# Moving the out-projection's weight preparation from SyncE's DMA queue to GpSimd's in a hybrid decoder layer

## The chip, the cores and the metric

The kernel runs on one core of a Trainium2 chip. A core has TensorE (matrix products), VectorE, ScalarE and GpSimd, and SyncE, which here does nothing but issue DMAs. In the profile they are PE (PEld for its weight loads), DVE, ACT, POOL and SP; "SPq" is SyncE's queue. DMAs are issued from SyncE's queue and, where they add to what is stored, from GpSimd's. The metric is the device time of one execution in microseconds (us): 1060.5 as the median of three runs, from 1057.32 to 1062.9.

## The reference

One layer on x of 1024 rows by 1024 columns, in float32. The rows are normalized and multiplied by one wide matrix w_in, whose columns give all inputs of two groups of heads. Eight heads of differential attention take the difference of two causal softmaxes over the values. Four heads of gated linear attention (GLA) run in chunks of 64 rows. Each head's output is normalized and gated, and both groups lie side by side as 2048 columns that w_out takes back to 1024:

```
h = rms_norm(x, pre_g);  z = h @ w_in
qa, ka, va, ga, qb, kb, vb, gb, gk_low = split_columns(z)
oa = rms_norm(diff_attention(qa, ka, va, lam), subln_g) * (1 - lam_init) * silu(ga)
ob = rms_norm(gla_chunked(qb, kb, vb, log_a), gla_g) * silu(gb)
y = concatenate([oa, ob]) @ w_out
return x + rms_norm(y, post_g)
```

The change is about the last product, and there about the rows 1024 to 2047 of w_out, which belong to GLA ("wg" below), and the rows 0 to 1023, which belong to attention ("wo").

## The kernel before, in words

**Numbers.** Every float32 operand of a product is split in two, a rounded high part (a ScalarE copy or cast to the type float32r) and the rest (a VectorE subtraction), and a product is three products: high by high, low by high, high by low. So each operand needs one cast and one subtraction before TensorE may read it.

**Seven products instead of eight.** Both the projection with w_in and GLA's part of the out-projection cut their matrices into two by two blocks and use Winograd's scheme with seven block products, numbered 1 to 7. Some products take a block as it is (for w_out: 1, 2, 3), the others take sums of blocks (4, 5, 6, 7). The matching operands of the left side are `mixe[n]`: for GLA's outputs, n = 1, 2, 4 come straight from the heads, and n = 3, 5, 6, 7 are sums that are built in DRAM tensors `lefts[n]` by DMAs that add (lines 955 to 963 and `add_left`, line 978).

**Stages.** (1) x is loaded, normalized, transposed and split; the first columns of w_in are loaded beside it. `load_early` (line 235) loads two pairs of column blocks ahead; the pair 4 uses the buffer of pair 2, so its load waits until that has been read. (2) The projection is a list `order` of 196 steps, one block product of a pair of column blocks each; `go(n)` (line 681) runs n steps, and each step prepares the weights of the next ones (`make_weights`, line 288: the cast is line 325, the subtraction line 326), multiplies, and takes what is done through ScalarE and VectorE (`take`, line 357; the snapshot of a product that is used twice is line 437) to DRAM. (3) From step 86 on a second stream, `fill`, runs beside it, one yield a step: GLA, head by head (`gla`, line 854), and then `gla_sums` (line 982), which loads the sums `lefts[n]`, splits them and stores them as `mixe[n]`. Its buffers are six named ones (`k0`, `q0`, `k1`, `q1`, `ks0`, `ks1`), two for each of n = 5, 6, 3, and the same six later hold attention's k, q and ks. (4) Attention and the out-projection run together (`merge`, line 1118): the scores, the values, and `out_early` (line 1430), which multiplies GLA's outputs by the w_out blocks in 28 units j, seven block products of four row tiles each.

**The out-projection's weights** are prepared in stage 2 and 3, once in each step behind step 41 (`wo_step`, line 652):

- *Copies and sums.* `weight_sums` (line 593) makes the four sums of w_out blocks in DRAM, each in four row tiles k: a plain DMA copies one block into `wsd[n][k]` (line 601, from SyncE), and a DMA that adds puts the other one on top (`add_weights`, line 610, from GpSimd). Sums 6 and 4 add another sum, 5 and 6 of the same k.
- *Loads.* A list `wo_todo` of jobs: 12 blocks, 16 sums, 16 tiles of the wo rows, and 4 tiles of the left sum 7. A job loads 128 x 512 numbers into a buffer `wo_raw` (line 677, from SyncE), and two steps later ScalarE casts it (line 640, or 643 with a sign), VectorE subtracts in place (641, 644), and two DMAs store both parts (`wgd`, `wod`, or for the left sum `mixe` by `store_left`, line 646). Two tags share this out, `t4` and `gup`; a tag comes free two steps after its split, and one step after it from step 86 on, when `gup` is given to GLA's states.
- *Use.* `gla_weights(n)` (line 1061) loads the four parts of block n from `wgd` into buffers of the projection's left operand, which are free once the last product that reads them is done: blocks 2, 4, 1 and then 6 at the end of the projection (lines 1100 to 1106), and blocks 7 and 5 (at j = 8) and 3 (at j = 16) inside `out_early`, where the first four tiles of the wo rows follow at j = 20.

**What sets the order.** The code is traced in the order written, and a scheduler then orders each engine's queue: among the instructions whose inputs and buffers it expects to be there, the one traced first goes first. So an instruction that waits for nothing may go far ahead of its place in the code. Three things hold it back: a buffer that isn't free, `tc.keep_in_program_order(ins)`, which ties an instruction to the one traced before it on its engine, and `with tc.issue_after(ins):`, which puts what the block traces on the engine of `ins` behind `ins` in that engine's queue. A queue, once ordered, is served strictly in order on the chip: an instruction that waits holds up all behind it.

GpSimd's other work before attention is small: clearing constants, scaling tiles of x (line 492), one addition for the first operand (line 552), a mask for each half of each GLA head (line 873), and the DMAs that add. In attention it scales the second softmax (line 1223), gates the outputs (line 1315) and issues the adding DMAs of the results (lines 1476, 1496 and 1644).

Of the kernel before, what the change touches and what calls it, by code (L numbers as in the profile page):

```python
# [31 lines left out]
def hymba_kernel(  # L32
# [255 lines left out]
    def make_weights(i):  # L288
        p, n = order[i]
        if wide(p) and p % 2:  # L290
            ws[i] = ws_wide[p - 1, n]
            return
        if p in early and n < 3:
            src = early[p][n - 1]
        else:
            fetch_raw(p, n, i)
            if wide(p):
                (b11, b21), (b12, b22) = ([raws[q].get(kh) for kh in range(2)] for q in (p, p + 1))
            else:
                top, bot = raws[p][0], raws[p][1]  # L300
                b11, b12 = top[:, :, :P], top[:, :, P:]
                b21, b22 = bot[:, :, :P], bot[:, :, P:]


            def sub(dst, a, b):
                dve.tensor_tensor(dst, a, b, ALU.subtract)  # L306
                return dst

            if n == 5:
                src = sub(b11, b12, b11)  # L310
            elif n == 6:
                src = sub(b11, b22, b11)
            elif n == 4:
                src = sub(b21, b21, b11)
            elif n == 7:
                src = sub(b12, b22, b12)
            else:
                src = {1: b11, 2: b21, 3: b22}[n]
        if wide(p):
            w = [ap.tile([P, HB, 256], F32R, tag="ring", name="w", bufs=NRING) for _ in range(2)]  # L320
            ws_wide[p, n] = w
        else:
            w2 = ap.tile([P, 2, HB, P], F32R, tag="ring", name="w", bufs=NRING)
            w = [w2[:, 0], w2[:, 1]]
        act.copy(w[0], src)  # L325
        dve.tensor_tensor(w[1], src, fp(w[0]), ALU.subtract)  # L326
        ws[i] = w

# [264 lines left out]
    def weight_sums():  # L593

        adds = []
        for k in range(HB):
            for n, src, more in (
# [3 lines left out]
                sp.dma_start(wsd[n][k], src)  # L601
# [8 lines left out]
    def add_weights(n, k, more):  # L610
        pool.dma_start(wsd[n][k], more, accum_op=ALU.add, max_dma_last_dim=2048)
        summed.add((n, k))
# [9 lines left out]
    wo_open, wo_free, wo_now = [], {"t4": 0, "gup": 0}, [0]  # L622
# [29 lines left out]
    def wo_step():  # L652
# [3 lines left out]
        if wo_open and wo_open[0][0] <= now - 2:  # L656
# [3 lines left out]
            split(hi, lo, raw, -1.0 if (kind, n) == ("block", 2) else 1.0)  # L660
            if tag in wo_free:
                wo_free[tag] = now + len(wo_free)
# [8 lines left out]
        if tags and wo_todo and wo_ready(*wo_todo[0]):  # L671
# [5 lines left out]
            sp.dma_start(raw, wo_source(*job))  # L677
# [176 lines left out]
    def gla(g):  # L854

        u = None
        for half in range(2):
# [30 lines left out]
            if (g, half) == (3, 0):  # L888
                add_left(0, 3, 6)
            us = [u]  # L890
# [91 lines left out]
    def gla_sums():  # L982
# [4 lines left out]
        units, open_units = [(n, i) for i in range(2) for n in (5, 6, 3)], []  # L987
        add_left(1, 6, 5)
        for now in range(10):
            if now == 2:  # L990
                add_left(1, 3, 6)
            if open_units and open_units[0][0] <= now - 2:
# [7 lines left out]
            if units and (units[0][1] == 0 or now > 3):  # L1000
# [33 lines left out]
    del wo_free["gup"]  # L1034
# [26 lines left out]
    def gla_weights(n):  # L1061
        wg[n] = []
        for i in range(2):
# [4 lines left out]
            for t in range(2):  # L1068
                ins = sp.dma_start(fp(parts[t]), wgd[n][i][t])
                if n == 6:  # L1070
                    tc.keep_in_program_order(ins)
            wg[n].append(parts)
# [27 lines left out]
    for n in (2, 4, 1):  # L1100
        gla_weights(n)
# [4 lines left out]
    gla_weights(6)  # L1106
# [323 lines left out]
    def out_early():  # L1430
# [3 lines left out]
        for j, (n, i) in enumerate(U):  # L1434
# [6 lines left out]
            if j == 8:  # L1441
                gla_weights(7)
                gla_weights(5)
            if j == 16:
                gla_weights(3)
            if j == 20:
                for e in range(4):
                    weights(e)
# [259 lines left out]
```

## Time and profile before

| what | value |
|---|---|
| three runs, median | 1060.5 us |
| the profiled execution | 1057.74 us |
| its span, first to last instruction | 1056.0 us |
| mean granted TensorE clock | 0.967 |
| DMA packets, bytes, rate | 187379, 273.96 MB, mean 259 GB/s |
| SyncE's queue (hardware_dynamic) | 176480 packets, 253.00 MB, 72.3% of 16 engines |
| GpSimd's queue (software_dynamic) | 10816 packets, 19.93 MB, 11.8% of 16 engines |

A row of the timeline gives the start in us, the duration in us, the engine, the line of the kernel, and the operation with what it writes and reads; "x4" means four instructions merged, and brackets hold the idle time before it and what ended that. A row of the waits gives who waited for whom: us in total, how often, and the longest. A row of stretches gives the busy time of each engine with the number of instructions, the granted clock as a share of full speed, the share of the 16 transfer engines that was busy (it can pass 1 a little, since it is a sum of the times that packets took), and the rate. In the chain of waits each piece is followed back from the last instruction to what released it. DMA-issuing instructions of SyncE aren't counted as busy. An idle engine costs nothing unless it is the one that the others wait for.

### The profile page before, as it was taken

How to read it: one execution, taken by the hardware profiler on the slowest of the kernel's cores; microseconds unless marked ns; L12 is line 12 of the kernel's file. 1: busy time of each engine (PE TensorE's matmuls, PEld its weight loads, DVE VectorE, ACT ScalarE, POOL GpSimd, SP SyncE). 2: the span in 40 equal slices, each digit the busy share in tenths (PEclk: the TensorE clock that was granted, in tenths of full speed). 3: DMA queues.
4: the chain of work that ended last, by engine and by line, in shares of the span. 5: the costliest groups of instructions: out<-in, count | busy, mean ns of one | idle time of the engine just before them, and what ended most of it. 6: DMA issues, size and time to landing. Idle time of an engine off the chain costs nothing.

```text
span 1056.0 us, 16013 instructions
## 1 busy us (share of the span) xinstructions
PE 963.9 (91%) x5290; PEld 828.5 (78%) x5290; DVE 749.5 (71%) x1471; ACT 615.5 (58%) x1194; POOL 168.9 (16%) x182
## 2 busy tenths in 40 slices
PE   6759999999899998999998899818999999999997
PEld 5758988888789986998787787616888888888786
DVE  7856588889776674666765777406798888988555
ACT  8432265478357444535554775305688777887773
POOL 5420000000000010000200000001234334434311
PEclk9979999999999998999999999958999999999999
DMA  9984256867877987996979879999999999997667
GB/s 346 283 192 130 89 154 202 297 208 269 287 264 224 294 234 240 316 285 226 308 218 279 263 221 320 358 310 296 341 347 315 369 362 290 303 272 195 136 177 156
DMA packets 187379, 273.96 MB, mean 259 GB/s; under 512 B 19632, under 2 KB 98480, under 8 KB 187200
## 3 DMA queue, kind: packets, MB, share of 16 engines
q1 hardware_dynamic: 176480, 253.00, 72.3%
q0 software_dynamic: 10816, 19.93, 11.8%
q8 instruction: 42, 0.69, 0.3%
q14 instruction: 41, 0.34, 0.1%
HBM read 164.34 MB, written 122.16 MB: 271 GB/s over the span
## 4 chain that ended last, share of the span: by engine, by line
PE 50%; DMA 22%; DVE 10%; issue 7%; ACT 5%; SPq 3%; POOL 1%; DVEq 0%; ACTq 0%; POOLq 0%
PE x L127 10%; PE ypart L127 9%; PE y L127 6%; PE z L127 6%; PE sc L127 6%; PE yps L127 4%; PE po L127 4%; PE wtr L130 2%; DMA left_d<-go 2%; DMA w_early<-in_w_in_dram 2%; DMA wo_raw<-in_w_out_dram 2%; DMA wg_hi<-wg_d 2%; DMA wo_d<-wo_raw 2%; DVE w L326 1%; DMA mixe<-wo_raw 1%
## 5 line engine op out<-in xcount | busy, mean ns | idle before, releaser
L325 ACT CAST w<-w_raw 128x512 fp32r<-128x512 f32 (+1 forms) x164 | 111.1, 685 | 68.0 <-PE y L127 25.9
L326 DVE TENSOR_TENSOR w<-w_raw,w 128x512 fp32r<-128x512 f32 (+1 forms) x164 | 126.3, 778 | 30.8 <-ACT w L325 21.2
L1217 ACT ACTIVATE p<-p,stt 128x896 f32<-128x896 f32 (+7 forms) x128 | 99.3, 776 | 61.5 <-DVE stt L1207 59.6
L1207 DVE CUSTOM_DVE_ANT_0 p<-sc,maskt 128x512 f32<-128x512 f32 (+3 forms) x128 | 74.4, 585 | 48.4 <-PE sc L127 47.8
L127 PE MATMUL x<-s_hi,w 128*128 128x512 f32 x320 | 81.9, 399 | 9.7 <-ACT s L437 9.7
L306 DVE TENSOR_TENSOR w_raw<-w_raw 128x512 f32<-128x512 f32 (+1 forms) x96 | 76.1, 793 | 18.1 <-DMA w_raw<-in_w_in_dram 16.7
L437 ACT COPY s<-x 128x512 f32<-128x512 f32 x84 | 48.9, 583 | 68.0 <-PE x L127 65.7
L1223 POOL TENSOR_SCALAR p<-p,stt,lam 128x1024 f32<-128x1024 f32 (+3 forms) x64 | 56.8, 887 | 190.0 <-DVE stt L1222 186.6
L127 PE MATMUL sc<-ks,q 128*128 128x512 f32 (+1 forms) x192 | 66.8, 351 | 22.1 <-DMA ks<-k_d 22.1
L127 PE MATMUL z<-s_hi,w 128*128 128x512 f32 x320 | 81.5, 398 | 2.8 <-DVE c L450 2.8
L127 PE MATMUL y<-h_hi,w 128*128 128x512 f32 x320 | 81.7, 398 | 2.2 <-DVE w L326 1.9
L873 POOL TENSOR_SCALAR_AFFINE_SELECT gan<-gan 128x512 f32<-128x512 f32 x8 | 14.5, 1808 | 411.2 <-ACT gan L872 411.2
L127 PE MATMUL ypart<-wg_hi,m_in 128*128 128x512 f32 x224 | 73.8, 411 | 6.8 <-issue 6.8
L127 PEld LDWEIGHTS x<-s_hi,w 128*128 128x128 f32 x320 | 60.3, 191 | 24.4 <-ACT s L437 12.2
L640 ACT CAST wo_hi<-wo_raw 128x512 fp32r<-128x512 f32 x44 | 27.2, 619 | 87.6 <-DMA wo_raw<-in_w_out_dram 55.8
L127 PEld LDWEIGHTS z<-s_hi,w 128*128 128x128 f32 x320 | 60.4, 191 | 15.9 <-DVE c L450 3.6
L127 PEld LDWEIGHTS y<-h_hi,w 128*128 128x128 f32 x320 | 60.6, 191 | 15.4 <-DVE w L326 2.3
L641 DVE TENSOR_TENSOR wo_raw<-wo_raw,wo_hi 128x512 fp32r<-128x512 f32 x44 | 30.4, 691 | 59.6 <-ACT wo_hi L640 59.4
L127 PE MATMUL sc<-k,q 128*128 128x512 f32 (+1 forms) x192 | 69.7, 368 | 0.6 <-DVE stt L1207 0.6
L127 PE MATMUL x<-h_hi,w 128*128 128x512 f32 x160 | 41.6, 404 | 19.0 <-ACT w L325 19.0
L127 PEld LDWEIGHTS sc<-ks,q 128*128 128x128 f32 x192 | 36.7, 191 | 27.8 <-issue 22.3
L1266 DVE TENSOR_TENSOR wt_lo<-wtr,wt_hi 128x512 fp32r<-128x512 f32 (+1 forms) x80 | 50.5, 633 | 7.0 <-ACT wt_hi L1265 6.8
(242 smaller groups left out, 2395.9 us busy)
## 6 DMA issues: line engine op xcount, KB each, us to landing
w_raw<-in_w_in_dram SPq DMA_DIRECT2D x56, 512.0 KB, 5.2
m_in<-mixe SPq DMA_DIRECT2D x28, 512.0 KB, 7.0
q<-q_d SPq DMA_DIRECT2D x32, 256.0 KB, 6.5
k<-k_d SPq DMA_DIRECT2D x32, 256.0 KB, 7.4
ks<-k_d SPq DMA_DIRECT2D x64, 128.0 KB, 6.7
v<-v_d SPq DMA_DIRECT2D x16, 512.0 KB, 8.5
y_d<-yst POOLq DMA_DIRECT2D x32, 256.0 KB, 7.0
wo_raw<-in_w_out_dram SPq DMA_DIRECT2D x28, 256.0 KB, 3.5
```

Source lines behind the costliest of these rows:

```text
L127: tc.keep_in_program_order(pe.matmul(*a, **k))
L130: tc.keep_in_program_order(pe.transpose(dst, src, ident))
L306: dve.tensor_tensor(dst, a, b, ALU.subtract)
L325: act.copy(w[0], src)
L326: dve.tensor_tensor(w[1], src, fp(w[0]), ALU.subtract)
L437: act.copy(b[k], ps)
L640: act.copy(hi, src)
L641: dve.tensor_tensor(lo, src, fp(hi), ALU.subtract)
L1207: ins = dve.tensor_tensor_reduce(p[:, a:e], sc[:, : e - a], maskt[:, NZ + P - (e - a) :] if last else maskt[:, : e - a], 1.0, 3e38 if i == ...
L1217: act.activation(p[:, :n], p[:, :n], AF.Exp, bias=st[:, m : m + 1], scale=-1.0, accum_out=st[:, 2 + m : 3 + m],)
L1223: pool.tensor_scalar(p1[:, :n], p1[:, :n], st[:, 5:6], lam, ALU.mult, ALU.mult)
L1266: dve.tensor_tensor(lo[:, :n], pt[:, :n], fp(hi[:, :n]), ALU.subtract)
```

## The change

Four things are changed.

1. The copies of the weight sums (line 601), the adding DMAs (611), the loads of `wo_raw` (677) and the loads of blocks 2, 4, 1 and 6 (1069) are issued from GpSimd's queue. The first three stand inside `with tc.issue_after(last_cast[0])`, where `last_cast` is the latest cast of `make_weights` (line 325), a ScalarE instruction.
2. `gup` becomes two tags, so that with `t4` three loads can be under way until GLA starts. A split follows its load by three steps instead of two, a tag comes free one step after its split, and with more than one tag no load is made in every third step.
3. The left sums 5, 6 and 3 of the first half become six more jobs of `wo_todo`, in tiles of 128 x 512; `gla_sums` keeps the second half, with starts at its steps 1, 3 and 5 and splits three steps later, in nine steps instead of ten.
4. In `out_early` the loads of blocks 7, 5 and 3 are issued in halves at j = 8 and 9, 10 and 11, 16 and 17, and those of the wo rows one at a time at j = 20 to 23.

```diff
-        act.copy(w[0], src)
+        last_cast[:] = [act.copy(w[0], src).ins]
...
-                sp.dma_start(wsd[n][k], src)
+                with tc.issue_after(last_cast[0]):
+                    pool.dma_start(wsd[n][k], src)
...
     def add_weights(n, k, more):
-        pool.dma_start(wsd[n][k], more, accum_op=ALU.add, max_dma_last_dim=2048)
+        with tc.issue_after(last_cast[0]):
+            pool.dma_start(wsd[n][k], more, accum_op=ALU.add, max_dma_last_dim=2048)
...
     wo_todo += [("left", 7, k) for k in range(HB)]
-    wo_open, wo_free, wo_now = [], {"t4": 0, "gup": 0}, [0]
+    wo_todo += [("left", n, k) for n in (5, 6, 3) for k in range(2)]
+    wo_open, wo_free, wo_now = [], {"t4": 0, "gup0": 0, "gup1": 0}, [0]
...
-        if wo_open and wo_open[0][0] <= now - 2:
+        if wo_open and wo_open[0][0] <= now - 3:
...
-            split(hi, lo, raw, -1.0 if (kind, n) == ("block", 2) else 1.0)
+            split(hi, lo, raw, -1.0 if (kind, n) in (("block", 2), ("left", 6)) else 1.0)
             if tag in wo_free:
-                wo_free[tag] = now + len(wo_free)
+                wo_free[tag] = now + 1
...
-        if tags and wo_todo and wo_ready(*wo_todo[0]):
+        if tags and wo_todo and wo_ready(*wo_todo[0]) and (len(wo_free) == 1 or now % 3):
...
-            sp.dma_start(raw, wo_source(*job))
+            with tc.issue_after(last_cast[0]):
+                pool.dma_start(raw, wo_source(*job))
...
             if (g, half) == (3, 0):
                 add_left(0, 3, 6)
+                left_done.update(((5, 0), (6, 0), (3, 0)))
...
-        units, open_units = [(n, i) for i in range(2) for n in (5, 6, 3)], []
+        units, open_units = [(n, 1) for n in (5, 6, 3)], []
         add_left(1, 6, 5)
-        for now in range(10):
-            if now == 2:
+        for now in range(9):
+            if now == 1:
                 add_left(1, 3, 6)
-            if open_units and open_units[0][0] <= now - 2:
+            if open_units and open_units[0][0] <= now - 3:
...
-            if units and (units[0][1] == 0 or now > 3):
+            if units and (now in (1, 3, 5)):
...
-    del wo_free["gup"]
+    del wo_free["gup0"], wo_free["gup1"]
...
-    def gla_weights(n):
-        wg[n] = []
-        for i in range(2):
+    def gla_weights(n, engine=sp, halves=(0, 1)):
+        for i in halves:
...
-                ins = sp.dma_start(fp(parts[t]), wgd[n][i][t])
+                ins = engine.dma_start(fp(parts[t]), wgd[n][i][t])
...
     for n in (2, 4, 1):
-        gla_weights(n)
+        gla_weights(n, pool)
...
-    gla_weights(6)
+    gla_weights(6, pool)
...
-            if j == 8:
-                gla_weights(7)
-                gla_weights(5)
-            if j == 16:
-                gla_weights(3)
-            if j == 20:
-                for e in range(4):
-                    weights(e)
+            for k, m in ((8, 7), (10, 5), (16, 3)):
+                if j in (k, k + 1):
+                    gla_weights(m, halves=(j - k,))
+            if 20 <= j < 24:
+                weights(j - 20)
```

3 lines of the change are left out of this document (2 added, 1 removed).

## The prediction

> **What bounds the kernel now.** First the page's busy line and slices, which say where TensorE rests.
>
> ```profile
> PE 963.9 (91%) x5290; PEld 828.5 (78%) x5290; DVE 749.5 (71%) x1471; ACT 615.5 (58%) x1194; POOL 168.9 (16%) x182
> ...
> PE   6759999999899998999998899818999999999997
> ...
> PEclk9979999999999998999999999958999999999999
> ```
>
> Each digit is 26.4 us (the clock's digits begin right behind its name). TensorE is busy 91% of the span; it rests in the first three slices and in one near 700 us. The same by stretches (columns: width, then PE, PEld, DVE, ACT and POOL busy, granted clock, DMA share, GB/s):
>
> ```profile
> 105.60:400.00 294.40, 290.25 (x1645) 254.90 (x1644) 223.70 (x350) 160.85 (x273) 5.96 (x4) 1.00 0.73 229
> 400.00:640.00 240.00, 225.37 (x1262) 194.86 (x1261) 162.59 (x250) 129.94 (x232) 17.71 (x12) 0.98 0.86 262
> ...
> 680.00:720.00 40.00, 11.58 (x29) 8.44 (x28) 5.07 (x10) 2.45 (x4) 0.00 (x0) 0.54 0.94 317
> 720.00:1056.00 336.00, 324.27 (x1681) 271.65 (x1680) 264.74 (x714) 250.53 (x564) 112.05 (x122) 1.00 0.91 274
> ```
>
> So three places can move: the start; the projection from 105.6 to 640 (294.4 - 290.25 = 4.2 and 240 - 225.4 = 14.6, together 18.8 us of rest); and the **seam** to attention at 680 to 720 (28.4 us of rest, at a granted clock of 0.54). Attention rests 11.7 us in 336. What TensorE waited for, the longest rows of each place (total, times, longest):
>
> ```profile
> PE x L127 <- ACT w L325: 19.0, 1, 19.0
> ```
> ```profile
> PE x L127 <- ACT s L437: 9.7, 5, 3.1
> ```
> ```profile
> PE sc L127 <- DMA ks<-k_d: 22.1, 2, 21.6
> PE ypart L127 <- issue: 6.8, 1, 6.8
> ```
>
> At the start the cast of line 325 stands in front of a load; in the projection snapshots (line 437) come late; at the seam the first scores wait 21.6 us for ks. Who issues what: the instructions that write ws_d (duration min/median/max in ns, first and last start in us), and the SyncE queue's timeline at both places (start, us, merged rows):
>
> ```profile
> L601 SPq DMA_DIRECT2D ws_d<-in_w_out_dram x16: 490/596/1667, 18.8 to 34.0; - x16
> ...
> L611 POOL DMA_DIRECT2D ws_d<-in_w_out_dram x8: 802/914/1682, 29.2 to 43.8; - x8
> ```
> ```profile
> 34.64 9.37 SPq L1452 DMA_DIRECT2D out_dram<-in_x_dram  x6
> 45.56 2.45 SPq L246 DMA_DIRECT2D w_early<-in_w_in_dram  x2
> ```
> ```profile
> 668.06 0.33 SPq L1069 DMA_DIRECT2D wg_hi<-wg_d  x1
> 668.70 0.37 SPq L1005 DMA_DIRECT2D left<-left_d  x1
> ...
> 680.41 1.54 SPq L1095 DMA_DIRECT2D m_in<-mixe  x2
> ...
> 695.67 0.53 SPq L1069 DMA_DIRECT2D wg_hi<-wg_d  x1
> ...
> 697.72 7.27 SPq L377 DMA_DIRECT2D q_d<-qk_st  x8
> ...
> 710.18 5.07 SPq L1026 DMA_DIRECT2D ks<-k_d  x8
> ```
>
> Two things are to be seen. What has no input is issued as soon as its queue is free: the copies of the weight sums, which the code writes behind step 41 of 196, go at 18.8 us, and the copies of line 1452, written inside attention, at 34.6. And at the seam ks stands last in a queue that issues without a pause.
>
> **The change, part by part.**
>
> *Does "behind casts" hold?* The helper that queues work behind an instruction ties only instructions of that instruction's own engine. Every older use in the kernel (lines 255, 1157, 1205, 1288, 1487, 1636) names one of the same engine; line 255 nests two, for ScalarE and VectorE. The new uses name a ScalarE cast around a GpSimd DMA, so I read them as empty. Then the copies go as soon as GpSimd is free, and its timeline says when that is:
>
> ```profile
> 2.19 0.28 POOL L75 TENSOR_SCALAR_AFFINE_SELECT maskt<-maskt 128x128 f32<-128x128 f32 x1
> ...
> 23.79 5.47 POOL L492 TENSOR_SCALAR xt<-xt,ssq 128x1024 f32<-128x1024 f32 x4 [2.26 <-ACT h_hi L531]
> 29.19 2.73 POOL L611 DMA_DIRECT2D ws_d<-in_w_out_dram  x3
> ...
> 67.83 3.33 POOL L611 DMA_DIRECT2D ws_d<-ws_d  x4
> ```
>
> So they start at 2.5 us beside the loads of x and w_in, not at 18.8.
>
> *Start.* The chain of waits, the sizes (KB each, us to landing) and three stretches:
>
> ```profile
> 30.32 0.87 PE xT L130 x8
> ...
> 45.56 18.15 DMA w_early<-in_w_in_dram
> ...
> 64.40 4.69 PE x L127 x12
> ```
> ```profile
> w_raw<-in_w_in_dram SPq DMA_DIRECT2D x56, 512.0 KB, 5.2
> ...
> ws_d<-in_w_out_dram SPq DMA_DIRECT2D x16, 256.0 KB, 7.5
> ```
> ```profile
> 20.00:25.00 5.00, 5.00 (x43) 5.00 (x42) 5.00 (x12) 4.17 (x9) 2.74 (x3) 1.00 1.10 374
> ...
> 60.00:65.00 5.00, 0.60 (x2) 0.50 (x3) 0.62 (x2) 1.27 (x3) 0.00 (x0) 0.50 1.00 282
> 65.00:70.00 5.00, 5.00 (x17) 3.98 (x16) 5.00 (x9) 3.11 (x6) 3.06 (x5) 0.70 0.28 64
> ```
>
> The DMA share is at its full value until 65 us and then falls to 0.28: the backlog ends just when the second w_early lands (45.56 + 18.15 = 63.7), and TensorE goes on at 64.4. Loss: the 16 copies of 256 KB are 4.2 MB, which at 374 GB/s delay x and w_in by 11 us if all stand ahead of them, by none if none do; I take 6, the middle. Gain: on a clear queue w_early would take the 5.2 us of a w_raw load of twice its size, 13 us less. But the bytes stay the same, and the late adds (67.8 us) now come earlier too, so the gain lies between 0 and 13; I take 3, because the backlog should empty about when it did. Net **+3**, with ends at -13 and +11.
>
> The Trainium skill says in "DMA: Bandwidth & Descriptors" (SWDGE vs HWDGE vs iDMA) that DMAs of GpSimd and of SyncE feed different internal queues of each transfer engine, served in turn. No run here shows that yet; by that rule x would have half the rate while copies stand, the loss would be nearer to 11 than to 0, and the start would cost about 8 instead of 3.
>
> *Projection.* What ScalarE waited for between 105 and 640 us, and the split of one block (durations in ns):
>
> ```profile
> ACT wo_hi L640 <- DMA wo_raw<-in_w_out_dram: 55.8, 14, 7.1
> ...
> ACT wo_hi L640 <- DMA wo_raw<-ws_d: 14.8, 5, 7.1
> ```
> ```profile
> L640 ACT CAST wo_hi<-wo_raw x44: 602/621/625, 178.9 to 591.4; 128x512 fp32r<-128x512 f32 x44
> L641 DVE TENSOR_TENSOR wo_raw<-wo_raw,wo_hi x44: 678/692/697, 179.6 to 592.0; 128x512 fp32r<-128x512 f32 x44
> ```
>
> ScalarE stands 70.6 us in front of raw blocks that come late, and behind it stand the snapshots that TensorE waits for. The load now has three steps of lead for two, one more buffer until GLA, and a queue without SyncE's stores ahead of it. Price: 16 copies, 54 loads (the 48 of before and six new left ones) and 16 weight loads of the seam are 86 issues more on GpSimd, at the 0.91 us of line 611 some 79 us, on an engine busy 168.9 of 1056. That is hidden as long as nothing useful waits in the queue. What stands behind a load that waits for its buffer are the eight masks of GLA (line 873), read five steps of that stream later, and the sums of the left blocks:
>
> ```profile
> 639.12 1.14 POOL L980 DMA_DIRECT2D left_d<-left_d  x1 [7.46 <-DMA left_d<-left_d]
> ```
>
> The last of these is read by the left load at 668.70, so 29 us of cover stand there. Gain: from 0 to all 18.8 us of rest; a loss isn't excluded if masks come late, with the same amount as its bound. The waits on line 437 are half of the rest (9.7), and not all are raw's; I take **-6**. With one buffer (from GLA on) a turn takes four steps for three, but more turns are done before GLA: the same work. The six left jobs moved to this stream are six casts of 0.62 us and six subtractions of 0.69 in place of three twice as wide: nothing, beside 225 us of TensorE in 240.
>
> *Seam.* Between 668.06 and 680.41 SyncE issues twelve block loads and one left load (0.37): 12.0 us go; the four from 695.67 to 697.72 are 2.0. If ks keeps its place it goes 14 us sooner. If it may also pass the q and k stores, since the left block that held its buffer no longer follows another one there, all of 21.6 + 6.8 = 28.4 us can go. Against that stand the bytes:
>
> ```profile
> 680.00:700.00 20.00, 8.20 (x21) 5.68 (x19) 3.61 (x6) 1.52 (x3) 0.00 (x0) 0.59 1.03 375
> 700.00:720.00 20.00, 3.38 (x8) 2.76 (x9) 1.46 (x4) 0.93 (x1) 0.00 (x0) 0.50 0.85 259
> ```
>
> To 700 us the transfer engines are full. Only behind that is there room: 375 - 259 GB/s over the 16 us to ks are 1.9 MB, 5 us. So the gain is 5 to 28; I take **-12**, near the issues taken away. Late next are block 2's weights and the first m_in for ypart, then v.
>
> The same page says, in Issuing engines are not separate DMA queues, that all DMAs share the 16 engines and a second issuer saves only issue time. The share of 1.03 up to 700 agrees; by it alone the seam gives 5 and not 12.
>
> *Later blocks in halves.* The issues of blocks 7, 5, 3 and of the rows are spread over the next units; each is read two units of work or more later, and attention rests 11.7 us in all: 0. Were a half late, it would cost a landing, some 5 us.
>
> **Sum.** 3 - 6 - 12 + 0 = -15. The profiled run took 1057.74 us (the span of 1056.0 and 1.7 around it), so 1042.7; it lies 2.8 under the median of 1060.5, and the forecast for the median is **1045 us**.
>
> **Rivals.**
>
> *The order holds after all*, and the copies go behind step 41. For it speaks the plain wording of the edit, against it that the engines differ. The start then loses nothing and gains most of 13, say 12: -12 - 6 - 12 = -30, 1030 us. Chance 0.12.
>
> *The seam is bound by bytes*, and who issues is nothing. For it: 375 GB/s; against: 259 at the end. Seam -5, the start +3, and a projection that the sooner writes slow, -3: -5, 1055 us. Chance 0.22, half "faster", half "same".
>
> *GpSimd's queue stalls the start*, and it ends slower. The adds wait for their copies, and adds onto sums for earlier adds. If most are queued ahead of the scaling of x tiles 4 to 7 (23.79; TensorE transposes them at 30.32), the scaling waits for the backlog. Ended at about 60 instead of 64, it would put the transposes 30 us late, less 5 to 13 regained at w_early: +17 to +25, about +21. With -6 and -12 that is +3, with the seam at its 5 us +10: 1064 to 1071. It decides from the point where the start costs more than 18. Against it: before, the adds stand behind that scaling (29.19). Chance 0.20.
>
> *The forecast*: 0.46, with an own range of 1035 to 1054.
>
> **How the numbers follow.** About 0.5% is what a measurement can tell from no change: 1055.2 and 1065.8. Faster 0.46 + 0.12 + 0.11 = 0.69, same 0.11, slower 0.20. The range reaches into both far rivals, and leaves out the lower part of the first and the upper part of the last: 1027 to 1068.
>
> **What would show it.** Start: line 601 on GpSimd before 20 us, the scaling of xt later than 23.8, TensorE's restart near 67; if line 601 first goes behind 100 us, the order held. Projection: ScalarE's wait at line 640 under 20 us. Seam: no line 1069 on SyncE before 700 us, and the first score 12 us sooner after the last projection product. The forecast is wrong if a mask or a left sum becomes what TensorE waits for, if the start's backlog lasts beyond 75 us, or if ks still stands last at the seam.

## The result: 0.9% slower, and the profile after

The changed kernel takes 1068.86 us (median of 12 runs, 1061.52 to 1074.52), the kernel before 1058.32 in the same comparison (12 runs, 1054.94 to 1062.9): a ratio of 1.0091, with an interval of 1.0063 to 1.012. The profiled execution took 1062.62 us, 6.2 less than the median; a second profile, below, shows which stretch differs between two executions.

First the page of the changed kernel: busy times, TensorE's slices (26.5 us each) and the transfer engines' slices.

```profile
PE 968.8 (91%) x5290; PEld 831.7 (78%) x5290; DVE 747.9 (71%) x1474; ACT 617.6 (58%) x1197; POOL 207.9 (20%) x268
...
PE   3869999989998999999999989574999999999997
...
DMA  9984246877997869888989759998999999997667
```

GpSimd has 86 instructions more, as counted. TensorE begins later (a 3 where a 6 stood), and the hole near 700 is shallower but wider: 5, 7, 4 for 8, 1, 8. To see what is gained and lost, the span is cut at two places that every version of this kernel has: the first of GLA's products (`pa`) and the end of the last one (`gms`). Stretches of the kernel before, with the columns of the prediction's:

```profile
0.00:300.90 300.90, 268.97 (x1496) 234.03 (x1497) 227.99 (x367) 156.79 (x268) 32.92 (x44) 0.97 0.74 227
300.90:616.80 315.90, 300.26 (x1834) 266.72 (x1834) 210.18 (x319) 169.24 (x297) 20.42 (x13) 0.98 0.84 259
616.80:1056.00 439.20, 394.64 (x1963) 327.75 (x1961) 311.35 (x786) 289.47 (x630) 115.55 (x125) 0.96 0.92 282
```

The same stretches of the changed kernel:

```profile
0.00:309.60 309.60, 273.34 (x1496) 236.98 (x1497) 226.54 (x367) 158.08 (x268) 54.22 (x87) 0.97 0.74 229
309.60:621.70 312.10, 299.57 (x1833) 266.40 (x1834) 209.64 (x320) 170.02 (x299) 27.79 (x37) 0.99 0.83 256
621.70:1060.60 438.90, 395.86 (x1962) 328.33 (x1961) 311.67 (x787) 289.56 (x632) 125.92 (x144) 0.96 0.91 281
```

TensorE's products agree to one (1496, 1833, 1962), so these are the same pieces of work. The way to GLA takes 8.7 us more, GLA's stretch 3.8 less in this execution, and all that follows takes 438.9 us for 439.2, although at the seam inside it the wait for ks went. That last pair of numbers is the first to explain.

**The seam.** What TensorE waited for from 640 us on, in the changed kernel:

```profile
PE ypart L127 <- DMA m_in<-mixe: 16.5, 2, 14.3
PE x L127 <- ACT s L439: 11.8, 1, 11.8
PE sc L127 <- DMA ks<-k_d: 2.7, 2, 1.9
```

The 21.6 us for ks are 1.9; instead a snapshot is 11.8 us late ahead of them, and an m_in 14.3 us behind them. The queues show why, GpSimd's, ScalarE's and SyncE's in turn:

```profile
653.88 1.09 POOL L1075 DMA_DIRECT2D wg_hi<-wg_d  x2 [3.64 <-PE x L127]
...
666.54 0.53 POOL L1075 DMA_DIRECT2D wg_lo<-wg_d  x1 [1.37 <-PE x L127]
```
```profile
677.39 1.04 ACT L645 CAST left_hi<-left 128x1024 fp32r<-128x1024 f32 x1 [12.70 <-DMA left<-left_d]
```
```profile
659.20 0.45 SPq L1012 DMA_DIRECT2D left<-left_d  x1
...
660.33 13.07 SPq L652 DMA_DIRECT2D mixe<-left  x2
...
704.93 5.04 SPq L379 DMA_DIRECT2D k_d<-qk_st  x8
...
720.53 0.54 SPq L1101 DMA_DIRECT2D m_in<-mixe  x1
```

A left load is issued at 659.20, in the middle of the twelve block loads (6 MB) that GpSimd now issues between 653.88 and 667.07, and it lands at 677.4, after 18 us; ScalarE stands in front of its cast, and the snapshot behind it. Later the third m_in is issued at 720.53, behind 24 stores of q and k. One long wait for ks has become two, for other loads.

**The start.** The copies' row, the first raw load, then SyncE's first loads of w_in, ScalarE near 61 us and TensorE near 66:

```profile
L604 POOL DMA_DIRECT2D ws_d<-in_w_out_dram x16: 526/558/1098, 2.2 to 34.7; - x16
```
```profile
3.50 0.60 POOL L683 DMA_DIRECT2D wo_raw<-in_w_out_dram  x1
```
```profile
3.22 8.35 SPq L204 DMA_DIRECT2D w_raw<-in_w_in_dram  x2
```
```profile
61.46 0.62 ACT L325 CAST w<-w_early 128x512 fp32r<-128x512 f32 x1 [3.19 <-DMA w_early<-in_w_in_dram]
...
62.93 0.68 ACT L533 ACTIVATE h_hi<-xT,pre_g 128x512 fp32r<-128x512 f32 x1
```
```profile
66.07 3.76 PE L127 MATMUL y<-w,h_hi 128*128 128x256 f32 x16 [7.14 <-DVE s L577]
```

The copies go from 2.2 us on, so the helper's block was empty, as read. The first three raw loads go among them, at 3.50 to 6.18 us; before, SyncE issued them among its copies, at 19.48 to 24.57 us. Two loads of w_in hold SyncE's queue 8.35 us, and the first product comes at 22.65 us (13.59 before). What sets the end of the stage stands in ScalarE's queue: a cast of w_early that waits for its load is now ordered in front of the last activations of h (62.93), and TensorE rests 7.1 us for what hangs on them. Pair 4 begins at 71.33 us for 64.40.

### The profile page after: what moved, and what is told of

It reads as the page before. It is cut to its first block, busy times and chain, and to the rows that moved or that the text cites. A ratio compares the mean times of both kernels' runs of the same rounds, so it can differ in the third digit from the quotient of the medians.

```text
span 1060.6 us, 16114 instructions
## 1 busy us (share of the span) xinstructions
PE 968.8 (91%) x5290; PEld 831.7 (78%) x5290; DVE 747.9 (71%) x1474; ACT 617.6 (58%) x1197; POOL 207.9 (20%) x268
## 5 line engine op out<-in xcount | busy, mean ns | idle before, releaser
L127 PE MATMUL x<-s_hi,w 128*128 128x512 f32 x320 | 86.6, 416 | 24.0 <-ACT s L439 23.9
L127 PEld LDWEIGHTS x<-s_hi,w 128*128 128x128 f32 x320 | 62.5, 199 | 40.6 <-ACT s L439 27.8
L683 POOL DMA_DIRECT2D wo_raw<-in_w_out_dram x28 | 15.4, 552 | 326.4 <-DMA wg_d<-wo_raw 133.4
L645 ACT CAST wo_hi<-wo_raw 128x512 fp32r<-128x512 f32 x48 | 29.6, 619 | 80.6 <-DMA wo_raw<-in_w_out_dram 27.7
L646 DVE TENSOR_TENSOR wo_raw<-wo_raw,wo_hi 128x512 fp32r<-128x512 f32 x48 | 32.9, 688 | 58.6 <-ACT wo_hi L645 58.6
L127 PEld LDWEIGHTS ypart<-wg_hi,m_in 128*128 128x128 f32 x224 | 40.0, 194 | 22.1 <-issue 14.7
L1232 DVE SCALAR_TENSOR_TENSOR p<-p,stt,p 128x1024 f32<-128x1024 f32 (+3 forms) x64 | 52.8, 824 | 4.1 <-POOL p L1229 3.8
```

The lines of the kernel that those rows point to most:

```text
L127: tc.keep_in_program_order(pe.matmul(*a, **k))
L645: act.copy(hi, src)
L646: dve.tensor_tensor(lo, src, fp(hi), ALU.subtract)
L1232: dve.scalar_tensor_tensor(p0[:, :n], p0[:, :n], st[:, 4:5], p1[:, :n], ALU.mult, ALU.subtract)
```

## The experiments

The first theory after these traces: GpSimd's copies cost the start, its block loads cost the end of the projection, and its raw loads are what helps (ScalarE's waits for raw blocks between 105 and 640 us, those for left blocks counted in both, fell from 76.8 us to 42.9; without them from 70.6 to 34.9). The rival: the timetable of the casts costs, whoever issues. Both were wrong on the raw loads. Medians (of 4 to 12 runs), ratios to the kernel before as it was timed beside each, with their intervals, and the three stretches of each profile (to GLA, GLA, the rest), us:

| kernel | median | ratio | to GLA | GLA | rest |
|---|---|---|---|---|---|
| before | 1058.3 | | 300.9 | 315.9 | 439.2 |
| after | 1068.9 | 1.0091 [1.0063, 1.012] | 309.6 | 312.1 | 438.9 |
| after_again | one run: 1072.1 | | 309.7 | 321.9 | 438.5 |
| wg_on_sync | 1071.4 | 1.0125 [1.0092, 1.0158] | 309.4 | 316.9 | 442.8 |
| copies_on_sync | 1064.4 | 1.0056 [1.0035, 1.0076] | 304.2 | 319.8 | 437.6 |
| copies_late | 1063.9 | 1.0052 [1.0027, 1.0077] | 301.1 | 317.3 | 437.6 |
| m_in_early | 1067.4 | 1.0089 [1.0061, 1.0116] | 309.0 | 317.9 | 444.5 |
| raw_on_sync | 1044.1 | 0.9859 [0.9829, 0.9889] | 302.2 | 304.7 | 439.7 |
| all_on_sync | 1052.9 | 0.9934 [0.9911, 0.9957] | 304.4 | 307.3 | 440.1 |
| raw_on_gpsimd_in_gla | 1058.0 | 0.9989 [0.9964, 1.0013] | 301.1 | 312.6 | 439.9 |
| seam_spread | 1045.6 | 0.986 [0.982, 0.9899] | 304.3 | 304.2 | 440.6 |
| seam_bytes | 1034.1 | 0.9788 [0.9755, 0.982] | 300.2 | 302.5 | 429.9 |
| copies_in_gap | 1023.1 | 0.9671 [0.9641, 0.9701] | 283.8 | 298.9 | 438.3 |
| before_copies_late | 1059.9 | 1.0013 [0.9993, 1.0032] | 301.7 | 315.3 | 440.8 |
| before_copies_on_scalar | 1059.6 | 1.0005 [0.9985, 1.0025] | 299.9 | 319.6 | 438.7 |
| before_copies_in_gap | 1041.7 | 0.9832 [0.9795, 0.9869] | 279.4 | 313.4 | 438.2 |
| before_wg_on_gpsimd | 1064.9 | 1.0068 [1.0041, 1.0095] | 300.9 | 317.5 | 444.6 |

Executions of one kernel lie up to 14 us apart, and a profile is one of them. It lies 4 to 9 us under its kernel's median in `after`, `copies_late` and `before_copies_in_gap`, and 4 to 6 us over it in `raw_on_sync`, `seam_spread` and `m_in_early`. So a stretch is read where several kernels agree on it, and a verdict from the medians.

### Undoing one queue at a time

`wg_on_sync`, blocks 2, 4, 1 and 6 back on SyncE:

```diff
-        gla_weights(n, pool)
+        gla_weights(n)
...
-    gla_weights(6, pool)
+    gla_weights(6)
```

> The changed kernel with one part undone: blocks 2, 4, 1 and 6 are loaded from SyncE again. Theory (6 MB of blocks from GpSimd at 654 to 667 us take the transfer engines from the last left load, whose cast holds ScalarE and so the projection): ScalarE's longest wait at the left cast falls from 12.7 us to under 6, the rest of TensorE inside the projection by about 10 us, and the seam grows back by 10 or more; the total stays within 5 us of the changed kernel's 1069. Rival (the left load is late by its own chain of adding DMAs): the wait of 12.7 stays above 9 and only the seam grows, 1075 to 1080.

From 600 us on, ScalarE's wait for the left loads and TensorE's longest:

```profile
ACT left_hi L645 <- DMA left<-left_d: 5.7, 2, 3.8
```
```profile
PE ypart L127 <- DMA m_in<-mixe: 31.3, 2, 20.8
```

The longest of ScalarE's waits for a left load fell from 12.7 to 3.8 us, as the theory had it, and the waits for m_in took its place (20.8 and 10.5): the stretch behind GLA is no shorter, 442.8 us. That these loads delay the left load is confirmed; that this costs time is not.

`copies_on_sync`, the copies alone back:

```diff
-                with tc.issue_after(last_cast[0]):
-                    pool.dma_start(wsd[n][k], src)
+                sp.dma_start(wsd[n][k], src)
```

> The changed kernel with the 16 copies issued from SyncE again (the adding DMAs stay on GpSimd, where they always were). Theory (the copies from GpSimd at 2.2 us take half the rate from x and w_in, and the start costs 7 us): the first product starts at 13.6 us and not at 22.7, the first product of pair 4 at 64 and not at 71, and the total falls by about 7, to 1062. Rival (the start is bound by all its bytes and the order is nothing): pair 4 starts at 69 to 72, the total stays at 1069.

The first product comes at 13.98 us and pair 4 at 65.83 again; the median falls by 4.5 us, for the 7 expected, and stays over the kernel before.

`raw_on_sync`, the raw loads alone back:

```diff
-            with tc.issue_after(last_cast[0]):
-                pool.dma_start(raw, wo_source(*job))
+            sp.dma_start(raw, wo_source(*job))
```

> The changed kernel with the raw loads alone back on SyncE's queue, behind SyncE's stores. Theory (GpSimd's queue for the raw loads is the part that helps, since ScalarE's waits for raw blocks fell from 70.6 to 43 us): those waits rise again by 10 us or more, TensorE's rest between 400 and 640 us goes from 9 back toward 14, and the time rises by 0 to 5 us. Rival (the third buffer and the third step of lead are what helped, and raw loads on GpSimd's queue only compete with the loads that SyncE issues): ScalarE's waits stay under 45 us, and the projection becomes as short or up to 4 us shorter.

The theory expected a loss of 0 to 5 us; it gains 24.7 and beats both kernels, far more than the rival's 4. ScalarE's waits for raw blocks, counted in the same way, are 46.5 us: most of that fall came with the timetable, not with the queue. Its three stretches, its first product and the start of its pair 4:

```profile
0.00:302.20 302.20, 270.40 (x1496) 233.70 (x1496) 229.06 (x373) 161.82 (x275) 40.46 (x60) 0.99 0.77 237
302.20:606.90 304.70, 297.36 (x1833) 266.84 (x1834) 205.61 (x315) 166.27 (x291) 18.01 (x13) 0.99 0.84 260
606.90:1046.60 439.70, 395.38 (x1963) 328.91 (x1961) 311.44 (x787) 289.71 (x632) 124.89 (x141) 0.96 0.92 280
```
```profile
26.15 4.24 PE L127 MATMUL x<-w,h_hi 128*128 128x256 f32 x16 [12.54 <-ACT h_hi L533]
...
61.15 1.19 PE L127 MATMUL x<-h_hi,w 128*128 128x512 f32 x4
```

By the profiles the gain is 7.4 us at the start and 7.4 in GLA's stretch; the rest of the 24.7 lies between these two executions and their medians. In GLA's stretch of each kernel, TensorE's waits for snapshots, the casts of raw blocks (count, busy and mean, then ScalarE's idle time before them, from 300 to 632 us), and the raw loads from issue to landing, in the changed kernel and then in this one:

```profile
PE x L127 <- ACT s L439: 7.7, 4, 3.8
```
```profile
L645 ACT CAST wo_hi<-wo_raw 128x512 fp32r<-128x512 f32 x26 | 16.1, 620 | 57.6 <-DMA wo_raw<-in_w_out_dram 23.9 <-DMA wo_raw<-left_d 8.0 <-issue 7.3
```
```profile
wo_raw<-in_w_out_dram POOLq DMA_DIRECT2D x16, 256.0 KB, 3.7
```
```profile
PE x L127 <- ACT s L439: 0.6, 1, 0.6
```
```profile
L645 ACT CAST wo_hi<-wo_raw 128x512 fp32r<-128x512 f32 x24 | 14.8, 618 | 41.4 <-DMA wo_raw<-in_w_out_dram 21.5 <-DMA wo_raw<-left_d 11.7 <-issue 3.2
```
```profile
wo_raw<-in_w_out_dram SPq DMA_DIRECT2D x16, 256.0 KB, 3.1
```

Issued from GpSimd, the same 256 KB land 0.6 us later there (1.2 over the whole run, 4.5 for 3.3), ScalarE stands 16 us longer in front of the casts, and the snapshots stand behind ScalarE. That this is the path to TensorE is argued: the snapshots' row falls by 7.1 us, but rows of 3.7 (z) and 3.3 (pa) stand in its place here. With the new timetable and SyncE's queue GLA takes 305 us where the old timetable took 316. The Trainium skill says in "DMA: Bandwidth & Descriptors" (Issuing engine by pattern) that DMAs issued from Sync are generally faster and those from GpSimd more flexible. These rows agree, 3.1 us against 3.7.

`raw_on_gpsimd_in_gla`, `raw_on_sync` with the raw loads on GpSimd again from the point where GLA begins:

```diff
-            sp.dma_start(raw, wo_source(*job))
+            (pool if len(wo_free) == 1 else sp).dma_start(raw, wo_source(*job))
```

> The changed kernel with the raw loads on SyncE's queue until GLA's stream begins and on GpSimd's from there on. Theory (the start lost 10 us by the three raw loads that go there at 3.5 to 6.2 us, and the stretch of GLA loses 10 us by the rest, whose landing takes 4.5 us after the issue from GpSimd for 3.3 from SyncE): pair 4 starts at 61 to 65, GLA's first product comes near 302, its stretch takes 314 to 320 us, and the time is 10 us above 1044, about 1054. Rival (what is lost in GLA comes from a start that runs late, or from the split of the loads in all stages): the stretch stays at 305 to 309 and the time within 4 us of 1044.

Pair 4 comes at 60.17, GLA at 301.1, and its stretch takes 312.6 us: 7.9 more, at the place expected, and the median is 13.9 higher, for 10 expected. So the raw loads on GpSimd's queue cost twice: 7 to 8 us ahead of GLA when they begin at 3.5 us beside the copies, and in GLA's stretch 8 us by this profile, more by the median. All profiles of that stretch with the new timetable agree: 312.1 to 321.9 us in the seven with the raw loads on GpSimd, 298.9 to 307.3 in the five with them on SyncE.

`all_on_sync` returns copies, raw loads and blocks to SyncE and leaves the timetable, the buffers, the left jobs and the halves (the edits are those of the three kernels above).

> The changed kernel with copies, raw loads and the loads of blocks 2, 4, 1 and 6 back on SyncE's queue; of the change there remain the adds' place, the third buffer and the timetable of raw loads and splits, the six left jobs moved, and the halves. Theory (the queue that issues is what lengthens the start and the left load): the first product comes at 14 us and pair 4 at 65 as in the kernel before, the left load lands within 4 us of need, and TensorE waits for no snapshot over 5 us near 680; the seam has the 22 us wait of before again; time within 3 us of the kernel before. Rival (the timetable itself costs the projection: fewer steps in which a load may be made, splits in bunches): the span from pair 4 to the last projection product stays above 624 us (before 619.2), and the time stays 4 us or more above the kernel before.

The timetable isn't what costs: it gains 5.8 us on the kernel before (1058.7 in that comparison), with GLA's stretch at 307.3. And `raw_on_sync`, which differs from it by the copies and blocks on GpSimd, is 8.8 us faster still. So those two gain here, while the copies cost 4.5 us beside raw loads in the same queue (`copies_on_sync`): what a move to GpSimd is worth depends on what else goes there.

`after_again`, the changed kernel once more.

> The changed kernel as it is, for a second profile, since the first one (1062.62 us) lies 6 below its median. Theory (from the profiles of its neighbours, which have the raw loads on GpSimd too: from the first to the last of GLA's products they take 317 to 320 us, the profile of the changed kernel only 312): this profile shows about 317 there, with the start and the time from GLA's end to the end of the span as before, 309 and 439 within 2 us. Rival: the 6 us lie at the start or behind GLA.

```profile
0.00:309.70 309.70, 273.26 (x1497) 236.06 (x1497) 226.10 (x367) 157.40 (x267) 55.38 (x87) 0.97 0.74 227
309.70:631.60 321.90, 301.79 (x1833) 268.02 (x1834) 209.37 (x320) 169.72 (x299) 27.55 (x37) 0.98 0.81 250
```

The place is right and the amount larger: the start repeats within 0.1 us and the rest within 0.4, and GLA's stretch is 9.8 us longer than in the first profile. The median of 1068.9 lies between the two. Nothing is gained in that stretch, then: 312 to 322 us in the changed kernel, for 316.

### Is the seam's wait worth anything?

`before_wg_on_gpsimd` makes only the seam's part of the change, in the kernel before:

```diff
-    def gla_weights(n):
+    def gla_weights(n, engine=sp):
...
-                ins = sp.dma_start(fp(parts[t]), wgd[n][i][t])
+                ins = engine.dma_start(fp(parts[t]), wgd[n][i][t])
...
-        gla_weights(n)
+        gla_weights(n, pool)
...
-    gla_weights(6)
+    gla_weights(6, pool)
```

> The kernel before with the loads of blocks 2, 4, 1 and 6 issued from GpSimd, and nothing else: the seam's part alone. Theory (from GLA's last product to the end of the span all kernels so far take 437.6 to 444.5 us, whoever issues, so the transfers of that stretch bound it): 436 to 444 us there, the wait for ks shrinks and another takes its place, and the time is within 4 us of the kernel before. Rival (the prediction's step: SyncE's 14 us of issues stand ahead of ks, and 12 us go with them): about 427 us there, and 1047 us in all.

```profile
PE sc L127 <- DMA ks<-k_d: 24.7, 2, 24.1
PE z L127 <- DVE c L450: 12.9, 2, 9.0
```

The wait for ks doesn't even shrink: 24.1 us, with 9 more in front of it. It ends 0.7% slower, at 1064.9, 6.9 us over the kernel before and past the 4 that the theory allowed; the prediction's 12 us are refuted for this part by itself.

`m_in_early`, in the changed kernel, issues four m_in loads ahead of the last stores in place of two:

```diff
-    load_left()
-    load_left()
+    for _ in range(4):
+        load_left()
```

> The changed kernel with all four first loads of m_in issued before the last steps of the projection instead of two, ahead of the last q and k stores in SyncE's queue. Theory (after the seam's ks wait went, the third m_in behind 24 stores is what TensorE waits for, 14.3 us): that wait falls below 4 us, and the time falls by 6 to 12 us against the changed kernel, to about 1058. Rival (the transfer engines are full there, so that two more megabytes ahead delay ks, k or q by as much): the first scores start 6 us or more later than in the changed kernel after the last projection product, and the time stays within 3 us of it.

The wait for m_in falls from 14.3 to 2.7 us, and waits of 6.9 and 5.1 us (snapshots), 4.6 (ks) and 9.0 (a probability tile) stand in TensorE's rows there; the median is 1.5 us under the changed kernel's. `seam_spread` does the same in `raw_on_sync` and moves blocks 1 and 6 into the out-projection:

```diff
-    for n in (2, 4, 1):
+    for n in (2, 4):
...
-    gla_weights(6, pool)
...
-            for k, m in ((8, 7), (10, 5), (16, 3)):
+            for k, m in ((1, 1), (3, 6), (8, 7), (10, 5), (16, 3)):
```

> The changed kernel with the raw loads on SyncE's queue (1044.1 us so far), and at the seam the loads of blocks 1 and 6 moved into the out-projection's units 1 to 4, issued from SyncE, and all four first m_in loads ahead of the last q and k stores. Theory (the stretch from GLA's end to the end of the span is bound by its transfers, whose bytes stay the same): the late left load of 11 us and the m_in wait of 8.7 us shrink, but other waits take their place; the stretch stays at 437 to 444 us and the time within 4 us of 1044. Rival (these waits are single late transfers, and nothing else is late behind them): the stretch falls below 432 us and the time to 1036 or less.

No gain: 1045.6 us, 440.6 behind GLA. `seam_bytes` is `raw_on_sync` with bytes taken away:

```diff
+                if n in (1, 6):
+                    pool.memset(fp(parts[t]), 0.0)
+                    continue
                 ins = engine.dma_start(fp(parts[t]), wgd[n][i][t])
```

> The changed kernel with the raw loads on SyncE's queue, and with the buffers of blocks 1 and 6 set to zero by GpSimd in place of being loaded: the products of these two blocks are zero, and 4.2 MB less is moved at the seam. Theory (from GLA's end on the transfers bound the time until about 760 us, at some 350 GB/s): the stretch from GLA's end to the end of the span falls from 439 to about 427 us, and the time from 1044 to about 1032. Rival (single late transfers in a row of waits bound it, not the bytes): the stretch stays within 4 us of 439.

```profile
602.70:1032.60 429.90, 395.45 (x1962) 329.49 (x1961) 311.87 (x787) 289.15 (x632) 126.53 (x141) 0.96 0.92 277
```

The stretch falls by 9.8 us and the time by 10. The mean rate is that of the other kernels (277 GB/s for 280), and 4.2 MB at 350 GB/s are 12 us. In the sixteen other profiles of the table, with fifteen arrangements of who issues what, this stretch took 437.6 to 444.6 us; the one kernel that took bytes away shortened it. So the bytes bound the seam inside it, as far as one such step can show; other amounts were not tried.

### Where the copies cost nothing

Three kernels move the copies (and the adds that follow them) out of the start. `copies_late` ties copies, adds and raw loads of the changed kernel behind a GpSimd instruction at 39.5 us, one of GpSimd's own, so that the tie holds:

```diff
+        gkl_set[:] = [pool.memset(fp(gkl), 0.0).ins]
...
-                with tc.issue_after(last_cast[0]):
+                with tc.issue_after(gkl_set[0]):
```

> The changed kernel with the order made real: copies, sums and raw loads stand behind a GpSimd instruction (the clearing of a buffer of the low-rank gate, at 63 us in the run after) in GpSimd's own queue, where naming a ScalarE cast has no effect. Theory: the first product starts at 13.6 us, the second w_early lands in some 6 us after its issue, pair 4 starts at 52 to 56 instead of 71, and the total falls by 15 to 19, to 1050 to 1054. Rival (the bytes of the start only move to where they cost the same): pair 4 sooner by 15, but the total within 5 of 1069.

`before_copies_late` ties the copies of the kernel before behind SyncE's latest load of w_in, so that they leave the start:

```diff
+                with tc.issue_after(last_raw[0]):
+                    sp.dma_start(wsd[n][k], src)
```

> The kernel before with one line more: the 16 copies stay on SyncE but are queued behind the latest load of w_in at their place in the code, so that they go from about step 41 on. Theory (the start is a backlog of transfers): the wait for w_early falls from 18 us to 8 to 12, since the copies of x to out stay ahead of it, and the total falls by 5 to 10, to 1048 to 1053. Rival (the projection pays for the bytes later): pair 4 sooner by as much, the total within 3 of 1058.

`before_copies_on_scalar` issues them from ScalarE's queue, behind the latest cast, which is the edit's wording made real:

```diff
+                with tc.issue_after(last_cast[0]):
+                    act.dma_start(wsd[n][k], src)
```

> The kernel before with the 16 copies issued from ScalarE's queue, each tied behind the latest weight cast, which is a tie on ScalarE's own engine: they go behind step 41 for certain, one in a step. The adds stay on GpSimd. Theory (the copies and adds cost TensorE where they come in a burst, and spread one to a step they are hidden): pair 4 starts near 47 us as when the copies were held back in a burst (46.7), the stretches from 160 to 320 us lose less than 5 us against the kernel before, and the time falls by 8 to 15 us, to about 1046. Rival (the projection is paced by all its transfers together, whatever their order, so what the start gains is lost later): the last projection product ends at 683 again and the time is within 4 us of the kernel before.

In all three pair 4 starts 18 to 19 us sooner than in the kernel before (45.2, 46.7, 46.6), and in all three GLA begins where it began (301.1, 301.7, 299.9). In `copies_late` the copies go within 17 us (40.4 to 57.7), and a load of w_in behind them took 21.3 us to land, for which TensorE rests 13.2. But a burst isn't all of it: the third kernel sends one copy a step, from 147.0 to 201.2 us, and loses as much. One stretch of it, and in the next fence the kernel before around that time:

```profile
185.00:205.00 20.00, 11.06 (x39) 8.72 (x40) 11.82 (x19) 5.60 (x10) 4.33 (x6) 0.81 1.07 327
```
```profile
105.00:145.00 40.00, 40.00 (x302) 38.34 (x301) 24.68 (x35) 13.88 (x20) 0.00 (x0) 1.00 0.37 111
145.00:205.00 60.00, 60.00 (x267) 49.67 (x266) 51.18 (x89) 32.29 (x55) 0.00 (x0) 1.00 0.74 222
```

From 147 us on, where both kernels made from the one before have them, the copies land on loads and stores that take 0.74 of the transfer engines already on the mean to 205 us; the share goes to 1.07, and TensorE rests 9 us in 20. Before that there is room: 0.37 from 105 to 145 us. `copies_in_gap` puts them there, in `raw_on_sync`:

```diff
-                    pool.dma_start(wsd[n][k], src)
+                    act.dma_start(wsd[n][k], src)
...
             if order[i][0] > EARLY:
                 wo_step()
+            elif i >= 14:
+                next(sum_steps, None)
```

> The changed kernel with the raw loads on SyncE's queue, and with the copies of the weight sums issued from ScalarE's queue, each tied behind the latest weight cast, one in a step from step 14 on: at about 65 to 130 us, where the transfer engines of the kernel before are busy only 0.36 to 0.43 of the time. Theory (copies and adds cost 17 us at the start and 17 us at 147 to 204 us, since the transfer engines are full at both places, and nothing where they have room): pair 4 starts near 47, GLA's first product comes at about 286 instead of 302, and the time falls by 12 to 17 us from 1044, to about 1030. Rival (something else paces the steps up to GLA, such as the loads of w_in behind the castings): GLA's first product stays at 299 to 302 as in the three runs with later copies, and the time stays within 4 us of 1044.

The copies' row, TensorE while they go, and the first two stretches:

```profile
L604 ACTq DMA_DIRECT2D ws_d<-in_w_out_dram x16: 497/507/878, 57.3 to 112.3; - x16
```
```profile
65.00:125.00 60.00, 59.06 (x434) 54.61 (x434) 39.43 (x58) 18.79 (x26) 11.44 (x14) 1.00 0.97 238
```
```profile
0.00:283.80 283.80, 267.60 (x1496) 232.61 (x1496) 230.46 (x372) 161.25 (x275) 33.06 (x44) 0.99 0.83 251
283.80:582.70 298.90, 294.24 (x1833) 264.19 (x1834) 206.40 (x315) 166.66 (x292) 17.11 (x13) 1.00 0.87 265
```

The share rises to 0.97, TensorE rests 0.9 us in 60, and GLA begins 18.4 us sooner. This is the best kernel of the study, 1023.1 us: 3.3% under the kernel before. `before_copies_in_gap` makes that one edit in the kernel before (the same lines, with the recording of `last_cast` that they need):

> The kernel before with one edit: the copies of the weight sums issued from ScalarE's queue, one in a step from step 14 on, where the transfer engines had room. Theory (the place of the copies is worth 17 us by itself, and adds to the 14 of the timetable): pair 4 starts near 46, GLA's first product comes near 284, its stretch takes 316 us as in the kernel before, 439 us follow, and the time is about 1041. Rival (the gain hangs on the third buffer and the longer lead, which took up the traffic): GLA's first product comes later than 292, and the time stays above 1050.

1041.7 us, 17 under the kernel before, as expected: the place of the copies is worth that much by itself. The 279.4 us to GLA in the table are from an execution of 1032.7, 9 under that median.

## Why the prediction was wrong, step by step

- *"Behind casts" is empty*: right. The copies go from 2.2 us on, and the first rival had nothing to stand on.
- *Start, +3*: the term was worked out for the copies, and for them it was near. In the four profiles that have the copies on GpSimd there and the raw loads on SyncE (`raw_on_sync`, `raw_on_gpsimd_in_gla`, `seam_spread`, `seam_bytes`) GLA begins at 300.2 to 304.3 us, for 300.9 before. What the sum put at nothing, without a reason, are the raw loads that go from GpSimd at the start too: with both, pair 4 comes 6.9 us later and GLA 8.7. The Trainium skill's rule in "DMA: Bandwidth & Descriptors" (SWDGE vs HWDGE vs iDMA), queues served in turn, made it 8 for the copies. The trace fits the rule in that SyncE's loads are late (8.35 us to issue two, for 2.22), but the copies alone didn't cost 8 in any run. And the first product doesn't set the end of the start: with the raw loads on SyncE it is later still (26.15) and pair 4 sooner (61.15), since ScalarE's order no longer has the cast of w_early ahead of h.
- *Projection, -6*: failed, in its assumption that a raw load is worth the same from either queue, "a queue without SyncE's stores ahead of it". The timetable and the third buffer took 9 to 11 us off GLA's stretch (`all_on_sync`, `raw_on_sync`: 307.3 and 304.7 for 315.9), and GpSimd's queue put 7 to 17 back (312.1 and 321.9 for 304.7). Of the named loss, late masks, there is no sign; the snapshots were late, as in the kernel before.
- *"29 us of cover" behind the last left sum*: wrong. It compared the sum with the left load's issue; that load then landed 18 us after its issue, among GpSimd's block loads. It belonged to the seam's bytes, and cost nothing beyond them (`wg_on_sync`).
- *Seam, -12*: failed, and it is the largest term that is missing. It weighed issues taken from SyncE against bytes and chose the issues. The wait for ks went, and the stretch behind GLA stayed (438.9 for 439.2). The rival that bytes bound the seam was right, further than it said: 0, not -5. By the Trainium skill's "DMA: Bandwidth & Descriptors" (Issuing engines are not separate DMA queues) the prediction made it 5. The rule pointed the right way, and here even the 5 were not to be had.
- *Halves, 0*: behind 745 us TensorE's longest wait is 1.5 us, for ScalarE; not tried by itself.
- *The sum*: +9 at the start, about 0 in GLA (between -4 and +6 in two profiles) and 0 behind it, in place of 3 - 6 - 12. The rival that GpSimd's queue stalls the start gave 1064 to 1071, and 1068.9 lies in it; but its mechanism, scaled tiles waiting for a backlog until 60 us, is not what happened (36.72 us in the trace).

**Still open**: why a load lands 0.6 to 1.2 us later from GpSimd's queue (the turn between queues or the work of issuing); which of the third buffer, the longer lead and the left jobs moved brings the 9 to 11 us in GLA's stretch, since no run parts them; and why GLA's stretch varies by 9.8 us between two executions of the changed kernel and not the rest. The start is long only where copies and raw loads both go from GpSimd (309 us to GLA; 304 with the copies on SyncE, 300 to 304 with the raw loads there); why ScalarE's order turns on that was not followed further.

## What to carry to other kernels

Before pricing a wait, cut the span where the same work begins and ends, and look at the transfer engines' share there: at 0.9 to 1.0 each wait that was removed here came back as another, and what was worth time was to take bytes away or to move them to where the share was low (0.37). A load that an engine waits for belongs in the queue that lands it soonest; "off the busy queue" is no gain by itself. A tie between instructions must be looked up in the trace: the first and last start of the tied line say whether it holds.

## What was unexpected of the hardware

- The same 256 KB load took 4.5 us (median of 28) from GpSimd's issue to landing and 3.3 from SyncE's, and in GLA's stretch alone 3.7 and 3.1; a 512 KB load among twelve of another queue took 18.
- SyncE's issue of two loads can take 8.35 us, for 2.22 when no other queue was loading.
- 16 copies and 16 adding DMAs, 8.4 MB, cost 17 to 18 us at a share of 0.74 or above, and nearly nothing at 0.37.
